# Eleven weight tiles of layer 1 split beside layer 0's output product and kept in DRAM, and norms without GpSimd

## The chip, the cores and the metric

The kernel runs on one core of a Trainium2 chip. The metric is the device time of one execution in microseconds. Before the change its median is 986.33 us over three runs (985.83 to 986.64). One further execution was profiled; all readings of the profile are from that one.

The core's engines are named as in the profile: PE is TensorE (PEld its weight loads), DVE is VectorE, ACT is ScalarE, POOL is GpSimd, SP is SyncE, which here only issues transfers. L12 is line 12 of the kernel before. Each engine runs its own instructions in order; an instruction that waits holds up what stands behind it on its engine.

## The reference

A decoder trunk of two layers on x of 1024 positions by 1024 channels, batch 1. Every layer is RMSNorm, a shift and scale computed from the conditioning vector c (adaLN), a mixer, a gate from c, and a residual add.

```python
# layer 0: gated multi-scale causal pooling, width 2048
u, z = split(h @ w_in, 2)
p = causal_multiscale_pool(u)                     # trailing means over 2, 4, 8, 16 minus u
y = einsum('bsgc,gcd->bsgd', p, w_group) * scale
x = x + gate * ((y * silu(z)) @ w_out)
# one K/V from the stream after layer 0, with a norm and shift/scale of its own
k, v = split(modulate(rmsnorm(x)) @ w_kv)
# layer 1: sliding-window attention (window 128), 16 heads on 2 K/V heads, sinks, T5 bias
q, z = split(h @ b_w_in, 2)
o = softmax_with_sink(q @ k.T / 8 + bias, masked) @ v
x = x + gate * ((o * silu(z)) @ b_w_out)
return rmsnorm(x, final_g)
```

The products have to be accurate to about float32. So the kernel splits every operand into a high part (rounded to the format fp32r that TensorE takes) and a low part, the remainder in the same format, and makes three matmuls for one: high by high, high by low, low by high.

## The kernel before

**Layout.** Channels lie on the 128 partitions and positions along the free axis, so x is eight tiles `xk[k]` of 128 by 1024. Positions are worked on in two halves q of 512. A weight tile is 128 by 1024 float32, 512 KB in DRAM: eight blocks of 128 by 128.

**Splitting a weight tile** is `load_w` (L133): `fetch` (L126) asks SP's queue for the tile into a `raw` buffer (two of them), `split_w` (L119) makes `wh`, the rounded copy, on ACT (L121) and `wl`, the remainder, on DVE (L123). `wh` and `wl` have two buffers each. A tile that is used for both halves of the positions in layer 1 is fetched and split twice.

**Layer 0's output product** (the loop over `order`, from L835) goes over 16 pairs (n, hf): eight output tiles n, each of two contraction halves hf. One step is 48 matmuls (8 blocks, 3 passes, both q) for n below `LATE` = 5, and 24 (q = 0 alone) for the rest; the q = 1 part of tiles 5 to 7 is done afterwards by `last_chunk`, in a plan by times. Beside the product lie the last adaLN dots, `ada_step` (L249): each of the 48 has one 512 KB load into a `tmp` buffer (three of them) on SP's queue and one DVE product with a sum (`ada_dot`, L238; the profile has two records for it, at L239). `ADA` says how many are written behind each step. Also beside it: parts of the gated activations come back from DRAM (`gather`), x is read again (`again_x`), and after the second half of each n `residual` (L684) and `square_add` (L197) run. For this loop the order is written for PE alone; on the other engines the framework's scheduler orders the work.

**Norms.** For a product's input x is multiplied by the reciprocal root `rb`, scaled and shifted and split. The class `Modulated` has two ways. `fold_h`/`fold_l` do it with two DVE instructions (L892, L898) and one ACT pass (L894); the first half of the positions uses it. The second half uses `step`: a DVE product (L177), an ACT pass for the high part (L159), an ACT pass in place (L163) and a POOL subtraction (L167). `prepare` (L1303) hands these steps out over time with gaps from `PREP`.

**Layer 1** is a list `specs` of products over one weight tile each: for either half q and each of four head groups r, two of queries and two of gates, then the output parts. Between them stands the attention of 32 blocks (`attend`, L1086): scores on PE, mask and maximum on DVE (L1107, L1111), exponentials on ACT (L1115), the division on DVE (L1119), transposes on PE (L1125), a cast on ACT and a remainder on DVE (L1128, L1129), two affine selects on POOL that cut the band (L1134, L1137, in 28 blocks), the product with V on PE (L1148, L1149), and the gating. `attend` is a generator, resumed by a modelled PE clock; between scores and transposes, and between transposes and the product with V, a lag of 6.0 us is written (`LAGS`). While one product runs, the next one's tile is loaded and split by `load_w`. PE's order is written; the others are scheduled by the framework. The last part of the output weights, `wbo[1]`, is used for q = 0 by `project_out(0, 1)` and once more by `out_quarter`, for which `load_last` (L1218) makes a second, lasting copy with its remainder on POOL. `stats` and `finish` make the last norm and write out.

Of the kernel before, what the change touches and what calls it, by code (L numbers as in the profile page):

```python
# [18 lines left out]
P = 128  # L19
D = 1024  # L20
T = 1024
H = 512
# [23 lines left out]
ADA = (0, 0, 0, 2, 4, 4, 4, 4, 4, 4, 1, 1, 1, 1, 0, 0)  # L46
# [9 lines left out]
def trunk(ctx, tc, xT, c, pack, ada_first, ada_rest, wu0_in, wg0_in, wa, wg, wao, wkv,  # L56
# [9 lines left out]
    pp = ctx.enter_context(tc.tile_pool(name="psum", bufs=1, space=PSUM))  # L66

# [67 lines left out]

    def rstd_stats(sq, n, more=None):
# [20 lines left out]

    def mod_h(xn, a, b, h):
        nc.scalar.activation(h, xn, AF.Identity, bias=b, scale=a)  # L159

    def mod_l(xn, a, b, h, l, f_eng=None, l_eng=None):
        if f_eng is nc.scalar:
            nc.scalar.activation(xn, xn, AF.Identity, bias=b, scale=a)  # L163
        else:
            nc.vector.tensor_scalar(out=xn, in0=xn, scalar1=a, scalar2=b,
                                    op0=ALU.mult, op1=ALU.add)
        (l_eng or nc.gpsimd).tensor_sub(out=l, in0=xn, in1=h.bitcast(F32))  # L167

    def split_mod(xn, a, b, h, l, f_eng=None):

        mod_h(xn, a, b, h)
        mod_l(xn, a, b, h, l, f_eng)

    def xn_tile(k, q, rb, xn=None):
        if xn is None:
            xn = sp.tile([P, H], F32, tag="xn", name="xn", bufs=5)
        nc.vector.tensor_mul(out=xn, in0=xk[k][:, half(q)], in1=rb)  # L177
        return xn
# [39 lines left out]
    with ExitStack() as sa:  # L218
# [580 lines left out]
        with tc.manual_schedule(engines={ET.PE}):  # L799
# [37 lines left out]
            ws, outs = {}, {}  # L837
            ws[0, 0] = half_w(0, 0)
            gather(4, 5, 6, 7)
            for i, (n, hf) in enumerate(order):  # L840
                if i + 1 < len(order):
                    ws[order[i + 1]] = half_w(*order[i + 1])
                if i == 0:
                    gather(8, 9)
                    new_x()
                    again_x(0)
                    gather(10, 11, 12, 13)
                elif i < 8:
                    again_x(i)
                qs = (0, 1) if n < LATE else (0,)  # L850
                if hf == 0:
                    outs[n] = [next_bank() for _ in qs]
                passes([(q, outs[n][q]) for q in qs], ws[n, hf], 0, g_acts(hf), KT,
                       hf == 0, hf == 1)
                for _ in range(ADA[i]):
                    ada_step()
                if hf == 1:
                    for q in qs:
                        residual(n, q, outs[n][q], 16)
# [572 lines left out]
```

## Time and profile before

| | |
|---|---|
| median of 3 runs | 986.33 us |
| the profiled execution's own time | 984.87 us |
| its span, first to last instruction | 982.6 us |
| granted TensorE clock | 0.996 |
| busy: PE, DVE, ACT, POOL | 961.9, 775.7, 458.1, 145.0 us |
| read from and written to HBM | 111.22 and 13.63 MB |
| output product of layer 0, as far as the loop goes | 423.69 to 565.13 us |
| attention layer | from about 600 us to the end |

The span is shorter than the execution's time by what lies before the first and after the last instruction. A matmul's end is modelled, so PE's busy time says where it stood still, but not how far it is from its peak. A wait is put down to the event that ended it.

### The profile page before, as it was taken

What the parts mean: (1) busy time and instruction counts of PE and PEld (TensorE: products, weight loads), DVE (VectorE), ACT (ScalarE), POOL (GpSimd) and SP (SyncE); (2) the same over time, 40 slices, a digit from 0 to 9 for tenths busy, and PEclk for the clock granted to TensorE, in tenths of its full rate; (3) what the DMA queues carried; (4) which work ended last, traced back from release to release, by engine and by line L of the source; (5) the groups of instructions that cost most, each with busy time, mean ns of one, the idle gap of its engine ahead of it and who ended that gap; (6) DMA issues with size and microseconds to landing.
All of it is one profiled execution on the core that took longest, in us unless ns stands there. A gap on an engine that the chain in (4) does not pass through costs nothing.

```text
span 982.6 us, 12696 instructions
## 1 busy us (share of the span) xinstructions
PE 961.9 (98%) x4538; PEld 801.2 (82%) x4538; DVE 775.7 (79%) x1411; ACT 458.1 (47%) x902; POOL 145.0 (15%) x173
## 2 busy tenths in 40 slices
PE   8999999999999999999999999999999999999996
PEld 6788888888888887888888888877888888887786
DVE  5897978677978699676782278599899878889985
ACT  6534434333433244551111145486677546566544
POOL 2100000000000000000000000052324313335723
PEclk9999999999999999999999999999999999999998
DMA  9453622264225411779861223222211221223222
GB/s 331 183 174 114 192 103 65 78 201 150 65 85 194 150 64 57 262 267 327 305 216 65 86 64 130 86 65 69 82 66 64 87 86 65 64 88 106 86 87 86
DMA packets 40625, 125.67 MB, mean 128 GB/s; under 512 B 4465, under 2 KB 6641, under 8 KB 40434
## 3 DMA queue, kind: packets, MB, share of 16 engines
q1 hardware_dynamic: 40416, 123.82, 37.6%
q10 hardware_dynamic: 146, 1.05, 0.3%
q8 instruction: 35, 0.57, 0.2%
q14 instruction: 28, 0.23, 0.1%
HBM read 111.22 MB, written 13.63 MB: 127 GB/s over the span
## 4 chain that ended last, share of the span: by engine, by line
PE 78%; DVE 16%; issue 2%; ACT 2%; POOL 1%; DMA 0%; POOLq 0%; DVEq 0%; SPq 0%; ACTq 0%
PE ps_d L214 14%; PE ps_S L214 9%; PE ps_d L636 9%; PE ps_d L203 6%; PE ps_d L204 6%; PE ps_d L205 6%; PE ps_S L636 4%; PE ps_o L214 4%; PE ps_tp L214 3%; DVE wl L123 2%; PE ps_d L374 2%; PE ps_o L636 2%; PE ps_tp L636 2%; DVE tmp L542 2%; PE ps_tp L1125 1%
## 5 line engine op out<-in xcount | busy, mean ns | idle before, releaser
L121 ACT CAST wh<-raw 128x1024 fp32r<-128x1024 f32 x73 | 76.5, 1048 | 101.4 <-PE ps_d L214 78.5
L123 DVE TENSOR_TENSOR wl<-raw,wh 128x1024 fp32r<-128x1024 f32 x73 | 94.2, 1290 | 26.7 <-ACT wh L121 22.8
L203 PE MATMUL ps_d<-hm,wh 128*128 128x512 f32 x288 | 113.8, 395 | 0.0
L205 PE MATMUL ps_d<-hm,wl 128*128 128x512 f32 x288 | 112.4, 390 | 0.3 <-DVE wl L123 0.3
L204 PE MATMUL ps_d<-hm,wh 128*128 128x512 f32 x288 | 112.4, 390 | 0.0
L239 DVE CUSTOM_DVE_ANT_0 tmp<-tmp,cact,pk 128x1024 f32<-128x1024 f32 x48 | 60.7, 1282 | 33.2 <-DMA tmp<-ada_rest 32.9
L214 PE MATMUL ps_d<-gh,wh 128*128 128x512 f32 x224 | 82.0, 389 | 0.0
L214 PE MATMUL ps_S<-gh,wh 128*128 128x512 f32 x192 | 64.5, 390 | 0.0
L205 PEld LDWEIGHTS ps_d<-hm,wl 128*128 128x128 f32 x288 | 54.1, 188 | 12.6 <-DVE wl L123 1.1
L636 PE MATMUL ps_d<-hs,ws 128*128 128x512 f32 x264 | 63.4, 389 | 0.0
L1115 ACT ACTIVATE pt<-pt,nm 128x129 f32<-128x129 f32 x128 | 50.2, 394 | 26.8 <-DVE nm L1111 24.6
L203 PEld LDWEIGHTS ps_d<-hm,wh 128*128 128x128 f32 x288 | 54.1, 188 | 10.2
L204 PEld LDWEIGHTS ps_d<-hm,wh 128*128 128x128 f32 x288 | 54.2, 188 | 10.0
L636 PEld LDWEIGHTS ps_d<-hs,ws 128*128 128x128 f32 x264 | 49.5, 188 | 10.3
L542 DVE TENSOR_TENSOR tmp<-tmp 128x1039 f32<-128x1039 f32 (+3 forms) x40 | 49.4, 1235 | 6.8 <-ACT tmp L672 5.7
L612 ACT CAST ws<-tw 128x512 fp32r<-128x512 f32 x44 | 26.8, 621 | 53.9 <-PE ps_tp L214 15.1
L636 PE MATMUL ps_d<-ha,ws 128*128 128x512 f32 x216 | 51.9, 389 | 0.0
L534 POOL MEMSET tmp<- 128x16 f32 x16 | 1.7, 111 | 331.4 <-DVE tmp L542 115.9
L214 PEld LDWEIGHTS ps_d<-gh,wh 128*128 128x128 f32 x224 | 42.1, 188 | 8.7
L636 PEld LDWEIGHTS ps_d<-ha,ws 128*128 128x128 f32 x216 | 40.5, 188 | 8.4
L147 POOL TENSOR_TENSOR rs<-v,mhalf 128x4 f32<-128x4 f32 (+1 forms) x7 | 8.2, 1164 | 241.6 <-DVE v L145 241.6
L214 PE MATMUL ps_d<-gh,wl 128*128 128x512 f32 x112 | 43.6, 389 | 0.0
(294 smaller groups left out, 2492.0 us busy)
## 6 DMA issues: line engine op xcount, KB each, us to landing
tmp<-ada_rest SPq DMA_DIRECT2D x48, 512.0 KB, 4.7
raw<-wb SPq DMA_DIRECT2D x32, 512.0 KB, 3.3
raw<-wa SPq DMA_DIRECT2D x28, 512.0 KB, 3.7
raw<-wao SPq DMA_DIRECT2D x20, 512.0 KB, 4.1
ad<-ada_first SPq DMA_DIRECT2D x16, 512.0 KB, 5.0
x<-xT SPq DMA_DIRECT2D x32, 256.0 KB, 5.9
raw<-wbo SPq DMA_DIRECT2D x16, 512.0 KB, 3.3
kept_g<-tmp SPq DMA_DIRECT2D x14, 512.0 KB, 2.9
```

What stands on the lines that cost most here:

```text
L121: nc.scalar.copy(out=wh, in_=raw)
L123: nc.vector.tensor_sub(out=wl, in0=raw, in1=wh.bitcast(F32))
L203: mm(ps, lh, acts(k, 0), start=k == 0, stop=False)
L204: mm(ps, lh, acts(k, 1), start=False, stop=False)
L205: mm(ps, ll, acts(k, 0), start=False, stop=k == n - 1)
L214: mm(p, lhs, acts(k, hl, q), start=start and k == 0 and s == 0, stop=stop and k == n - 1 and s == 2)
L239: nc.vector.tensor_tensor_reduce(out=raw, in0=raw, in1=ca, scale=0.5, scalar=pk[:, bcol:bcol + 1], op0=ALU.mult, op1=ALU.add, accum_out=ad ...
L374: mm(psu[i, q], w0[k // 2][:, k % 2, w, i * P:(i + 1) * P], block(k, q)[hl], start=k == 0 and s == 0, stop=k == KT - 1 and s == 2)
L542: nc.vector.tensor_add(out=nx[:, 2 * s - 1:], in0=cur[:, 2 * s - 1:], in1=cur[:, s - 1:PAD + T - s])
L612: nc.scalar.copy(out=ws[i][:, 0, :], in_=src)
L636: mm(ps, lhs, acts(k, hl), start=start and k == 0 and s == 0, stop=k == 3 and s == 2, skip_group_check=True)
L1115: nc.scalar.activation(pt[:, i, :P + 1], pt[:, i, :P + 1], AF.Exp, bias=nm[:, i:i + 1], scale=-1.0, accum_out=den[:, i:i + 1])
```

## The change

The diff has four parts.

- **The output product is cut in two.** The first six steps (`BESIDE`) stay as they were, with 24 adaLN dots written behind them instead of 10. For the last ten steps the order is now written for all five engines. In each, the next tile is split, the tile after it asked for, and then a few jobs follow from `JOBS`: an A is an adaLN dot, an S splits one of eleven tiles of `wb`. Both load into a `tmp` buffer on POOL's queue; three are asked for before the first is used, and each job that is done asks for one more. An S makes its high part in one of two `stage` buffers, its low part in place, and writes both to DRAM through POOL's queue (`keep`).
- **Layer 1 takes its tiles ready where they are kept.** `load_any` replaces `load_w`: a kept tile comes back as two transfers on POOL's queue, two products ahead instead of one, into pairs of buffers taken in turn from `raw`, `wh` and `wl`. A tile that is not kept is loaded by SP and split as before, and then kept through SP's queue, so that the second half of the positions finds it. `wbo[1]` is split once, into the lasting copy.
- **The norms of the second half** use `fold_h`/`fold_l`.
- **The output parts** come in another order: `project_out(1, 0)[:2]` before `project_out(0, 1)`, and `stats(0)` and `finish(0, 4)` one product later.

```diff
-ADA = (0, 0, 0, 2, 4, 4, 4, 4, 4, 4, 1, 1, 1, 1, 0, 0)
+ADA = (0, 0, 2, 6, 8, 8)
+BESIDE = 6
+JOBS = ("AAS", "AAS", "SSA", "SSA", "S", "S", "S", "S", "S", "")
...
+    def keep(key, hi, lo, queue=nc.sync):
+        kept_w[key] = [kp.tile([P, 1024], F32, name="kw") for _ in range(2)]
+        for dst, src in zip(kept_w[key], (hi, lo)):
+            queue.dma_start(dst, src.bitcast(F32))
+    def pair_tiles():
+        tags = (("raw", "raw"), ("wh", "wl"), ("wh", "wl"))[turns[0] % 3]
+        turns[0] += 1
+        return [wp.tile([P, 1024], F32R, tag=t, name="w2") for t in tags]
...
+            staged = [1, 8, 9, 2, 3, 10, 11, 4, 5, 12, 13]
+            def ask():
+                if not jobs:
+                    return
+                raw = tmp()[:, :1024]
+                kind = jobs.pop(0)
+                if kind == "A":
+                    i = rest_at[0]
+                    nc.gpsimd.dma_start(raw, ada_rest[i])
+                    rest_at[0] += 1
+                    asked.append(lambda: ada_dot(raw, cact, *rest_cols[i]))
+                else:
+                    i = staged.pop(0)
+                    nc.gpsimd.dma_start(raw, wb[i])
+                    asked.append(lambda: stage_split(i, raw))
+            def stage_split(i, raw):
+                hi = stage_hi[i % 2].rearrange("p a c -> p (a c)")
+                nc.scalar.copy(out=hi, in_=raw)
+                lo = raw.bitcast(F32R)
+                nc.vector.tensor_sub(out=lo, in0=raw, in1=hi.bitcast(F32))
+                keep(("b", i), hi, lo, nc.gpsimd)
...
+        with tc.manual_schedule(engines={ET.PE, ET.Activation, ET.DVE, ET.Pool, ET.SP}):
+            stage_hi = [slot("stage") for _ in range(2)]
+            raw = fetch(wao[order[BESIDE + 1]])
+            jobs, asked = list("".join(JOBS)), []
+            for _ in range(3):
+                ask()
+            for i in range(BESIDE, len(order)):
+                if i + 1 < len(order):
+                    ws[order[i + 1]] = split_w(*raw)
+                if i + 2 < len(order):
+                    raw = fetch(wao[order[i + 2]])
+                if i < KT:
+                    again_x(i)
+                for _ in JOBS[i - BESIDE]:
+                    asked.pop(0)()
+                    ask()
+                out_half(i)
...
+            if key in again:
+                keep(again[key], *w)
+        again = {"wk": ("kv", 0), "wv": ("kv", 1), "wq": ("b", 0)}
...
-    def load_last():
...
+    def load_any(key):
+        stays = key[0] == "o" and key[1] == 1
+        if stays:
+            t = hp.tile([P, 2, T], F32R, tag="h", name="wo")
+            w = t[:, 0, :], t[:, 1, :]
+            last_w.append(w)
+        else:
+            w = pair_tiles()
+        if key in kept_w:
+            for dst, src in zip(w, kept_w[key]):
+                nc.gpsimd.dma_start(dst, src)
+        else:
+            raw = bp.tile([P, 1024], F32, tag="raw1", name="raw1", bufs=2)
+            nc.sync.dma_start(raw, (wb if key[0] == "b" else wbo)[key[1:]])
+            nc.scalar.copy(out=w[0], in_=raw)
+            nc.vector.tensor_sub(out=w[1], in0=raw, in1=w[0].bitcast(F32))
+            if not stays:
+                keep(key, *w)
+        return w
...
             for k in ks:
-                m.step(k)
+                m.fold_h(k, sp.tile([P, H], F32, tag="xn", name="xn", bufs=5))
+                m.fold_l(k)
                 yield gap
...
-        *woven(project_out(0, 1) + project_out(1, 0)[:2], (0, 2, 4, 6)),
-        stats(0), project_out(1, 0)[2], finish(0, 4, FINISH[0]),
-        *project_out(1, 0)[3:],
+        *project_out(1, 0)[:2],
+        *project_out(0, 1),
+        project_out(1, 0)[2], stats(0), project_out(1, 0)[3], finish(0, 4, FINISH[0]),
+        project_out(1, 0)[4],
...
-        loaded = {srcs[0]: got["wq"]}
+        loaded = {srcs[0]: got["wq"], srcs[1]: load_any(specs[srcs[1]][0])}
...
-                nxt = srcs.index(i) + 1
+                nxt = srcs.index(i) + 2
                 if nxt < len(srcs):
-                    loaded[srcs[nxt]] = load_w(specs[srcs[nxt]][0])
+                    loaded[srcs[nxt]] = load_any(specs[srcs[nxt]][0])
```

More of the change, by code (lines that the diff above doesn't have):

```diff
@@ L156, in rstd_spread @@
         return bc
[L158 to L178, printed above, removed]
     sqh = [None, None]
@@ L1177, in run @@
                 yield from gemm_steps(w, i * 512, acts, 4, done)
-        return wbo[part, n2], run
+        return ("o", part, n2), run
     def bare(f):
```

70 lines of the change are left out of this document (24 added, 46 removed).

## The prediction

> **What bounds the kernel now.** I read the page first (sections 1 and 4), then the stages one by one, then the waits of TensorE, then the chain of waits inside the stages that lose time.
>
> ```profile
> span 982.6 us, 12696 instructions
> ...
> PE 961.9 (98%) x4538; PEld 801.2 (82%) x4538; DVE 775.7 (79%) x1411; ACT 458.1 (47%) x902; POOL 145.0 (15%) x173
> ...
> PE 78%; DVE 16%; issue 2%; ACT 2%; POOL 1%; DMA 0%; POOLq 0%; DVEq 0%; SPq 0%; ACTq 0%
> ```
>
> TensorE bounds the kernel, and its number of matmuls does not change. So the change can win only where TensorE waits, and it loses wherever it makes a new wait. The stages it touches are the output product of layer 0 (423.69 to 565.13) and layer 1 (from about 600):
>
> ```profile
> 423.69:488.97 65.28, 65.28 (x289) 54.05 (x288) 45.93 (x69) 16.44 (x25) 0.00 (x0) 1.00 0.90 313
> 488.97:532.49 43.52, 43.52 (x193) 36.04 (x192) 22.78 (x36) 6.75 (x9) 0.00 (x0) 1.00 0.50 165
> 532.49:565.13 32.64, 32.64 (x145) 27.03 (x144) 11.32 (x13) 7.43 (x9) 0.00 (x0) 1.00 0.25 81
> ...
> 600.00:640.00 40.00, 39.73 (x196) 33.35 (x195) 27.44 (x55) 20.88 (x41) 3.73 (x5) 1.00 0.36 118
> 640.00:690.00 50.00, 46.21 (x231) 38.09 (x230) 47.33 (x103) 36.91 (x78) 22.22 (x20) 1.00 0.23 74
> 690.00:740.00 50.00, 49.59 (x249) 41.28 (x248) 46.26 (x120) 37.95 (x89) 18.30 (x19) 1.00 0.23 74
> 740.00:880.00 140.00, 140.00 (x700) 118.14 (x699) 117.68 (x296) 83.99 (x211) 39.94 (x46) 1.00 0.22 72
> 880.00:935.00 55.00, 52.19 (x269) 43.28 (x268) 51.16 (x113) 31.95 (x77) 37.20 (x28) 1.00 0.31 96
> ```
>
> The columns are the stretch, its length, then busy time of PE, PEld, DVE, ACT and POOL, the granted clock, the DMA share and GB/s. The output product loses nothing: ten halves, of which the four from 488.97 take 10.88 us each (43.52 / 4) and the last six 5.44 (32.64 / 6), with DVE, ACT and the DMA engines half idle in them. Layer 1 loses 0.27 + 3.79 + 0.41 + 2.81 = 7.28 us of TensorE, and DVE is busy 95% and 93% just there. What TensorE waits for:
>
> ```profile
> PE ps_tp L1125 <- DVE pt L1119: 6.1, 5, 1.6
> PE ps_tp L154 <- DVE cur L1129: 0.4, 1, 0.4
> PE ps_d L205 <- DVE wl L123: 0.3, 1, 0.3
> PE ps_S L1105 <- DVE qt L1063: 0.3, 1, 0.3
> ```
>
> Eight waits, all for DVE, six of the seven us for the softmax division. The chain of waits from 640 to 690 and from 880 to 935 says what DVE did instead:
>
> ```profile
> by line: DVE wl L123 16.5%; DVE xn L177 12.4%; DVE pt L1111 8.8%; DVE ps_S L1107 7.0%; DVE cur L1129 6.9%; DVE pt L1119 6.7%; DVE of L1155 6.5%; issue 5.0%; POOL hm L167 4.8%; DVE qt L1063 4.1%; DVE qt L1161 3.2%; DVE of L1159 2.9%; DVE KL
> ...
> by line: DVE wl L123 14.7%; DVE of L1159 9.7%; DVE of L1155 8.6%; ACT pt L1115 8.3%; DVE cur L1129 7.4%; DVE x L686 7.4%; issue 6.1%; DVE pt L1111 5.6%; DVE ps_S L1107 5.5%; ACT wh L121 5.2%; DVE pt L1119 4.3%; DVE qt L1161 3.7%; DVE szb L1
> ```
>
> In both, the low half of a weight split (L123) is the largest item, 8.2 and 8.1 us, and the matmuls hardly appear: there the chain runs along DVE.
>
> **The change part by part.** *Splits leave layer 1.* Today layer 1 splits 45 tiles on DVE and four of wbo once more on POOL; afterwards 12 are split there (four of wb, the eight of wbo), and 33 come ready from DRAM as two transfers.
>
> ```profile
> L123 DVE TENSOR_TENSOR wl<-raw,wh 128x1024 fp32r<-128x1024 f32 x45 | 60.0, 1334 | 12.2 <-ACT wh L121 9.9 <-PE ps_o L1149 1.7
> L177 DVE TENSOR_TENSOR xn<-x,rb 128x512 f32<-128x512 f32 x16 | 12.5, 809 | 0.4 <-POOL hm L167 0.3
> L898 DVE SCALAR_TENSOR_TENSOR hm<-tmp,adac,hm 128x512 fp32r<-128x512 f32 x4 | 2.9, 744 | 0.0
> L1129 DVE TENSOR_TENSOR cur<-ps_tp,cur 128x512 fp32r<-128x512 f32 x32 | 22.1, 690 | 7.1 <-ACT cur L1128 6.3
> ...
> L121 ACT CAST wh<-raw 128x1024 fp32r<-128x1024 f32 x45 | 47.0, 1045 | 15.2 <-issue 7.6 <-PE ps_d L204 6.4 <-ACT qt L1062 0.9
> L1128 ACT CAST cur<-ps_tp 128x512 fp32r<-128x512 f32 x32 | 18.8, 587 | 11.0 <-PE ps_tp L1125 10.4
> ...
> L1134 POOL TENSOR_SCALAR_AFFINE_SELECT prev<-cur 128x1024 fp32r<-128x1024 f32 x28 | 33.3, 1189 | 46.8 <-DVE cur L1129 46.8
> L1137 POOL TENSOR_SCALAR_AFFINE_SELECT cur<-cur 128x1024 fp32r<-128x1024 f32 x28 | 32.5, 1160 | 1.8
> L167 POOL TENSOR_TENSOR hm<-xn,hm 128x512 fp32r<-128x512 f32 x16 | 22.4, 1403 | 24.9 <-ACT xn L163 22.6 <-DVE wl L123 2.3
> ```
>
> 33 x 1.334 = 44.0 us leave DVE, 33 x 1.045 = 34.5 us leave ACT. *The norms.* Each of the 16 tiles of normalized input had one DVE product (0.81), two ACT passes and one subtraction on POOL (1.40). It gets two DVE instructions of the kind of L898 (0.744 each, 1.49) and one ACT pass: DVE +0.68, POOL -1.40. Layer 1 as a whole loses 44.0 - 10.9 = 33 us of DVE work, but the two edits do not meet in the same place:
>
> ```profile
> 640.00:690.00 50.00, 8.62 (x6) 1.00 0.23 74
> 880.00:935.00 55.00, 9.79 (x7) 1.00 0.31 96
> ...
> 640.00:690.00 50.00, 10.40 (x13) 1.00 0.23 74
> ```
>
> (Busy time of L123 in the two stretches, then of L177 in the first.) From 640 to 690 six splits leave, 8.62 us, but 13 of the 16 norms lie there: 10.40 us become 13 x 1.49 = 19.4, so DVE gains 0.35 us of work, not relief. What does leave is POOL's subtraction, which stretches DVE's product:
>
> ```profile
> 644.76 1.77 DVE L177 TENSOR_TENSOR xn<-x,rb 128x512 f32<-128x512 f32 x1 [0.34 <-POOL hm L167]
> ...
> 642.35 3.64 POOL L167 TENSOR_TENSOR hm<-xn,hm 128x512 fp32r<-128x512 f32 x2 [7.06 <-ACT xn L163]
> ```
>
> Beside a POOL subtraction the DVE product took 1.77 us instead of its mean 0.81. The gain in this stretch lies between 0 (DVE as full as before) and 3.79; the chain gives up its 2.4 us of POOL (4.8%) and keeps the 0.35, so I take 1.5, nearer to zero because those 2.4 us overlap the stretched DVE instruction. From 880 to 935 three of seven splits leave (four tiles of wbo are still split there), 4.2 us, and POOL's four subtractions of those tiles move to ACT and DVE's ordinary split; a norm does not stand there. Of 2.81 I take 2.1 (bounds 0 and 2.81). The two neighbours: 0.5 of 0.68. Each wait also hides about 0.16 us under the modelled end of a matmul (0.39 shown, one issued every 10.88 / 48 = 0.227): 8 x 0.16, of which 0.4. Sum of the gain: **4.5 us** (0 to 7.3 + 1.3).
>
> *Reloads* cost layer 1 nothing if they are in time: a tile is asked for two products ahead (2 x 24 x 0.227 = 10.9 us at least), one transfer takes 3.3 us (row below), and 33 x 1.05 + 11 x 1.05 MB instead of 33 x 0.52 adds 29 MB to 380 us, 76 GB/s on top of 72 to 118. What they cost when POOL is late is the second rival.
>
> *The eleven tiles beside the output product.* Some prices, and how many dots DVE had done by 489 and in the 25 us after (a dot leaves two records):
>
> ```profile
> 423.69:489.00 65.31, 24.91 (x39) 1.00 0.90 313
> 489.00:514.00 25.00, 13.13 (x22) 1.00 0.74 244
> ...
> 495.27 1.21 DVE L123 TENSOR_TENSOR wl<-raw,wh 128x1024 fp32r<-128x1024 f32 x1
> ```
>
> From 488.97 on, every engine follows the written order: 17 jobs, 0 to 16, in the order A A S, A A S, S S A, S S A, S, S, S, S, S over nine halves. A is an adaLN dot (one load, one DVE dot), S a tile (one load, ACT copy 1.05, DVE subtraction 1.21 undisturbed, two writes). DVE has room: 11 x 1.21 = 13.3 us in 76. The DMA engines have little, and the POOL queue less. Bytes: 17 loads, 22 writes, 8 tiles of wao and 1 MB of x, 49 x 0.524 = 25.7 MB in 76.2 us, 337 GB/s. The most that the engines moved in any half of the product:
>
> ```profile
> 456.33:467.21 10.88, 10.88 (x49) 9.01 (x48) 7.83 (x13) 2.28 (x4) 0.00 (x0) 1.00 0.98 345
> ...
> raw<-wb SPq DMA_DIRECT2D x32, 512.0 KB, 3.3
> kept_g<-tmp SPq DMA_DIRECT2D x14, 512.0 KB, 2.9
> ```
>
> So one transfer occupies 0.524 / 345 = 1.52 us, and a write lands 2.9 - 1.52 = 1.38 after its bytes. Now the queue: loads and writes of the jobs all go through POOL, in order. There are three `tmp` buffers, all asked for ahead; the load asked after job j takes j's own buffer, so POOL stands until j's low half has landed, and the next tile's two writes stand behind it. One tile therefore costs a full cycle: load + two writes + landing, 3 x 1.52 + 1.38 = 5.9 us, and 7.5 when SP's tile of wao shares the engines (+1.52). That is over the 5.44 us of a late half, and S S A needs 13.4 to 16.4 against 10.88. Only the start made earlier can pay. Job 15 must be done before the last half's tile is split, and its load waits for the write of job 12: five cycles after the write of job 5 (jobs 6, 7, 9, 10, 12) plus the loads of 11 and 14 (3.0). Job 5's write lands at 509 at best: 499.85, when half 6 ends and frees a buffer, + split 2.26 + two dots of 1.28 + subtraction 1.21 + write 2.9. At worst DVE enters late: 24 dots stand ahead of the stage now, 20 were done by 489, and four more at the old pace (25 / 11 = 2.27) end at 498; split, two dots and job 2 with both its writes (1.2 + 2.6 + 2.3 + 4.4) give 508.5, job 5's load, split and writes (3.3 + 2.3 + 4.4) 518. Then load 3.3, copy 1.05, two subtractions 2.42. Best: 509 + 29.7 + 3.0 + 6.8 = 548.5, 11 us early, no stall. Worst by these rows: 518 + 37.3 + 3.0 + 6.8 = 565.1 against 560.1 (last half at 559.7, its low weights 0.4 later): 5.0 us of stall. I take **2.5**, the middle: the DMA share of the six halves before, 0.90, speaks for the long cycle, the loads made ahead for the short one.
>
> [...] No row of before has a transfer issued by POOL.
>
> What one POOL issue costs is bounded by POOL's rows: 0 and L167's 1.40 us. Inside a cycle the issues overlap the bytes, so the sum takes 0 and the third rival 1.40.
>
> **Sum.** 984.87 is the profiled execution's own time (982.6 + 2.27 around the span), 1.46 under the median 986.33. -4.5 + 2.5 = -2.0: 982.9 profiled, **984.3** by the median. That is the size of what this kernel's measurement tells from nothing (0.2%, 2 us).
>
> **The rivals.** *One, the stage hides it all:* the first writes land near 509 and the output product stalls nowhere. For it: 76 us in which DVE is 45% and ACT 19% busy. Against: 337 of 345 GB/s. 986.3 - 4.5 = 981.8. *Two, POOL in layer 1:* the 66 reloads stand in POOL's queue with the affine selects of the 28 masked blocks. A reload waits for the product before to free its buffers, and behind it stand L1134 and L1137, for whose 2.35 us the weighted values on TensorE wait; the slack is the written lag of 6.0 us less cast, subtraction and selects (0.59 + 0.69 + 2.35), 2.4. Two issues at 1.40 exceed it by 0.4: 5.6 us if half the blocks are hit, 984.3 + 5.6 = 989.9. For: POOL is busy 37 of 55 us from 880. Against: it loses L167's 22.4 us. *Three, slower, one mechanism:* each cycle of the stage carries one unhidden POOL issue. At 7.46 + 1.40 = 8.9 us the last tile is ready at 518 + 44.3 + 9.8 = 572.1, 12 us late; -4.5 + 12 = +7.5, **993.8**. It decides from a cycle of about 7.8, where the stall passes 6.5 and the sum passes +2.
>
> **How the numbers follow.** Forecast 0.35 (own range 981 to 987: 0.18 past 2 us faster, 0.16 within, 0.01 slower), rival one 0.22, two 0.15 (0.05 of it within, if few blocks are hit), three 0.23, something else 0.05 (0.02, 0.01, 0.02). Faster: 0.18 + 0.22 + 0.02 = 0.42. Same: 0.16 + 0.05 + 0.01 = 0.22. Slower: 0.01 + 0.10 + 0.23 + 0.02 = 0.36. The range takes in one with the upper bound of the gain and three: 977 to 995.
>
> **What would show it.** The windows of the last ten halves: PE busy below its length, first from the fifth half on, with waits for L123's or the stage's subtraction; POOL's waits there are for landings of the kept tiles, 6 to 7.5 us apart. In 640 to 690 DVE still over 90% and the wait for L1119 smaller by a third only; in 880 to 935 PE idle under 1 us. No L167, no L177. I am wrong if TensorE loses nothing before 600 (cycle shorter than 5.9), if 640 to 690 loses nothing (the port, not the work, was the limit), or if TensorE waits for a reload.

## The result, and the profile after

The changed kernel takes 1000.42 us (median of 5, 998.02 to 1002.21) against 986.64 for the kernel before (median of 5): a ratio of 1.0139, 95% interval 1.0123 to 1.0155. It is 1.4% slower where 0.2% faster was forecast, and outside the range. The profiled execution is the fastest of the five, 998.02. Medians and ratios below leave out one execution of the run with the norms alone, which took 3451.69 us at a granted clock of 1.00.

The page of the changed kernel, its span, busy time and chain by engine:

```profile
span 996.3 us, 12788 instructions
...
PE 965.5 (97%) x4538; PEld 803.8 (81%) x4538; DVE 748.5 (75%) x1405; ACT 422.2 (42%) x860; POOL 163.9 (16%) x258
...
PE 67%; DVE 14%; DMA 7%; issue 7%; ACT 2%; POOL 2%; POOLq 0%; SPq 0%; DVEq 0%; ACTq 0%
```

DVE lost 27 us of work, ACT 36, and the span grew by 13.7 us all the same. PE is busy 3.6 us longer with the same 4538 matmuls, so some of them ran slower. DMA, 0% of the chain before, is 7% of it now. By stretch (PE, PEld, DVE, ACT, POOL, then granted clock, DMA share, GB/s):

```profile
489.15:532.67 43.52, 43.52 (x193) 35.96 (x192) 24.72 (x32) 10.18 (x12) 10.49 (x19) 1.00 0.80 277
532.67:584.30 51.63, 38.21 (x145) 29.72 (x144) 21.21 (x22) 14.56 (x16) 10.77 (x20) 0.83 0.79 281
619.00:659.00 40.00, 40.00 (x197) 33.64 (x197) 22.56 (x51) 16.02 (x36) 9.35 (x17) 1.00 0.82 288
659.00:708.00 49.00, 48.00 (x242) 39.97 (x241) 43.98 (x112) 27.12 (x72) 17.28 (x27) 1.00 0.39 130
708.00:757.00 49.00, 49.00 (x246) 41.16 (x245) 46.76 (x116) 33.19 (x80) 10.93 (x14) 1.00 0.59 215
757.00:896.00 139.00, 138.53 (x693) 116.75 (x692) 98.86 (x282) 63.81 (x187) 53.45 (x76) 1.00 0.47 154
896.00:949.00 53.00, 51.02 (x262) 43.10 (x261) 39.94 (x111) 25.49 (x70) 26.50 (x28) 1.00 0.23 74
```

The four long halves of the output product still take 43.52 us. The six short ones take 51.63 instead of 32.64: **19.0 us lost**, 13.4 of them idle (51.63 - 38.21) and 5.6 in which PE is busy longer (38.21 - 32.64). Most of the 5.6 is matmuls that ran slower: the granted clock is 0.50 while PE works from 548.39 to 554.59 and from 578.48 to 581.90, and half of these 9.6 us is 4.8. The rest is not accounted for; modelled ends can hide some of it. Layer 1 from 619 on has 0 + 1.00 + 0 + 0.47 + 1.98 = 3.45 us of idle PE where the same stretches had 7.28. By the span it gives back 19.0 + 0.2 (the later start of the first of these halves) - 13.7 = 5.5 us, the rest of it under modelled ends and in the last norm.

What PE waits for, first from 489 to 585 and then from 600 to 960:

```profile
PE ps_S L211 <- ACT wh L126: 12.9, 2, 10.1
PE ps_S L211 <- DVE wl L128: 0.5, 1, 0.5
...
PE ps_tp L1158 <- DVE pt L1152: 2.7, 3, 2.0
PE ps_d L201 <- DVE hm L943: 0.8, 1, 0.8
```

In the stage it is two waits for the high half of an output weight (L126 is the split's cast, L121 before): 10.1 us before half 11, the second of the short ones, and 2.8 before half 15, the last. In layer 1 the softmax division, 6.1 us before, is down to 2.7. PE nowhere waits for a reload.

Why was that cast late? It stands in ACT's and DVE's written order behind the jobs of step 9 and the residual of half 9. DVE in time, around the 10 us wait (start, duration, instruction, idle before it):

```profile
541.69 1.23 DVE L858 TENSOR_TENSOR tmp<-tmp,stage 128x1024 fp32r<-128x1024 f32 x1 [5.08 <-ACT stage L856]
544.13 1.28 DVE L236 CUSTOM_DVE_ANT_0 tmp<-tmp,cact,pk 128x1024 f32<-128x1024 f32 x1 [1.22 <-DMA tmp<-ada_rest]
...
545.34 0.75 DVE L683 SCALAR_TENSOR_TENSOR x<-ps_o,adac,x 128x512 f32<-128x512 f32 x1
546.00 0.74 DVE L683 SCALAR_TENSOR_TENSOR x<-ps_d,adac,x 128x512 f32<-128x512 f32 x1
546.78 1.35 DVE L192 TENSOR_TENSOR sqh<-sqh,sq 128x512 f32<-128x512 f32 x2
548.38 1.23 DVE L128 TENSOR_TENSOR wl<-raw,wh 128x1024 fp32r<-128x1024 f32 x1 [0.24 <-ACT wh L126]
```

DVE has time, it idles 5.08 and 1.22 us. It waits for a staged tile (L858) and then for a dot's load; only after them come the residual, its squares (ACT's, ahead of L126) and the split. Both loads were late on POOL: the tile's, issued at 531.87 behind two writes, was there for its cast at 540.61, and the dot's was issued at 539.72, after POOL had stood still for 7.31 us. Some of POOL's transfers in time, POOL's waits for landings from 489 to 585, and the median time from issue to landing:

```profile
512.28 1.79 POOL L850 DMA_DIRECT2D tmp<-wb  x3 [8.13 <-DMA kw<-tmp]
...
539.72 0.55 POOL L845 DMA_DIRECT2D tmp<-ada_rest  x1 [7.31 <-DMA kw<-tmp]
...
564.58 0.55 POOL L850 DMA_DIRECT2D tmp<-wb  x1 [7.05 <-DMA kw<-tmp]
565.18 0.53 POOL L147 DMA_DIRECT2D kw<-stage  x1
565.78 0.53 POOL L147 DMA_DIRECT2D kw<-tmp  x1
574.13 0.55 POOL L850 DMA_DIRECT2D tmp<-wb  x1 [7.82 <-DMA kw<-tmp]
```

```profile
POOL tmp L850 <- DMA kw<-tmp: 30.7, 4, 8.1
POOL tmp L845 <- DMA kw<-tmp: 11.0, 2, 7.3
```

```profile
w<-kw POOLq DMA_DIRECT2D x66, 512.0 KB, 4.2
...
tmp<-wb POOLq DMA_DIRECT2D x11, 512.0 KB, 4.6
kw<-stage POOLq DMA_DIRECT2D x11, 512.0 KB, 6.0
kw<-tmp POOLq DMA_DIRECT2D x11, 512.0 KB, 7.2
```

Here is the predicted cycle: a load is issued when the low half of an earlier tile has landed, the next tile's two writes follow it at once, and POOL stands still again, for 7 to 8 us in five of the eight cases and for 3.7 to 5.5 in the others. From the load after the first write (512.28) to the load after the eighth (574.13) are seven cycles, **8.8 us each**. An issue takes 0.54 us, but the low half lands 7.2 us after its own, where 2.9 was put in.

### The profile page after: what moved, and what is told of

Same layout as the page of the kernel before. It is cut to its first block, busy times and chain, and to the rows that moved or that the text cites. A ratio compares the mean times of both kernels' runs of the same rounds, so it can differ in the third digit from the quotient of the medians.

```text
span 996.3 us, 12788 instructions
## 1 busy us (share of the span) xinstructions
PE 965.5 (97%) x4538; PEld 803.8 (81%) x4538; DVE 748.5 (75%) x1405; ACT 422.2 (42%) x860; POOL 163.9 (16%) x258
## 3 DMA queue, kind: packets, MB, share of 16 engines
q0 software_dynamic: 15120, 55.06, 16.4%
## 4 chain that ended last, share of the span: by engine, by line
PE 67%; DVE 14%; DMA 7%; issue 7%; ACT 2%; POOL 2%; POOLq 0%; SPq 0%; DVEq 0%; ACTq 0%
PE ps_d L633 9%; PE ps_d L200 8%; PE ps_d L201 8%; PE ps_d L202 8%; PE ps_d L211 7%; PE ps_S L211 5%; PE ps_S L633 4%; DMA tmp<-ada_rest 3%; PE ps_d L371 2%; PE ps_o L633 2%; PE ps_tp L211 2%; PE ps_tp L633 2%; DVE tmp L539 2%; PE ps_o L211 2%; DVE tmp L236 1%
## 5 line engine op out<-in xcount | busy, mean ns | idle before, releaser
L200 PE MATMUL ps_d<-hm,w 128*128 128x512 f32 x264 | 104.5, 396 | 0.0
L201 PE MATMUL ps_d<-hm,w 128*128 128x512 f32 x264 | 103.1, 391 | 0.8 <-DVE hm L943 0.8
L202 PE MATMUL ps_d<-hm,w 128*128 128x512 f32 x264 | 102.9, 390 | 0.0
L211 PE MATMUL ps_S<-gh,wh 128*128 128x512 f32 x192 | 68.0, 410 | 12.9 <-ACT wh L126 12.9
L202 PEld LDWEIGHTS ps_d<-hm,w 128*128 128x128 f32 x264 | 49.6, 188 | 10.6
L201 PEld LDWEIGHTS ps_d<-hm,w 128*128 128x128 f32 x264 | 49.7, 188 | 10.2 <-DVE hm L943 1.2
L200 PEld LDWEIGHTS ps_d<-hm,w 128*128 128x128 f32 x264 | 49.6, 188 | 9.2
L211 PEld LDWEIGHTS ps_S<-gh,wh 128*128 128x128 f32 x192 | 37.8, 199 | 21.6 <-ACT wh L126 13.7
L1262 POOL DMA_DIRECT2D w<-kw x66 | 35.8, 543 | 92.0 <-PE ps_d L202 56.0
L126 ACT CAST wh<-raw 128x1024 fp32r<-128x1024 f32 x28 | 29.4, 1050 | 38.7 <-PE ps_d L211 31.3
```

The lines of the kernel that those rows point to most:

```text
L126: nc.scalar.copy(out=wh, in_=raw)
L200: mm(ps, lh, acts(k, 0), start=k == 0, stop=False)
L201: mm(ps, lh, acts(k, 1), start=False, stop=False)
L202: mm(ps, ll, acts(k, 0), start=False, stop=k == n - 1)
L211: mm(p, lhs, acts(k, hl, q), start=start and k == 0 and s == 0, stop=stop and k == n - 1 and s == 2)
L1262: nc.gpsimd.dma_start(dst, src)
```

## The experiments

Every profiled stage length below runs from the start of half 6 to the end of half 15; it is 76.16 us in the kernel before.

**The writes on SP.**

```
-                keep(("b", i), hi, lo, nc.gpsimd)
+                keep(("b", i), hi, lo)
```

> The changed kernel with one word changed: the two writes of each staged tile go out on SP's queue, the loads stay on POOL's. Bytes, jobs and buffers are the same. Theory 1 (POOL's order): POOL stands for the landing of a tile's low half with the next tile's writes behind it, 8.1 + 3.7 + 7.3 + 7.7 + 7.1 + 7.8 us in the changed kernel. With the writes elsewhere a buffer's own round (load 4.2, copy 1.05, subtraction 1.22, writes about 5) is all that is left, some 12 us over three buffers, 4 us a tile, under the 5.44 of a late half: the 19.0 us that the ten halves lost fall to 0 to 4, and the time to 981 to 986. Theory 2 (bytes): 25.7 MB in 76 us is what the DMA engines carry at most, and who asks does not matter: at least 14 of the 19 us stay, 995 or more. Theory 3 (the place of the jobs in ACT's and DVE's order): the next half's split stands behind jobs whose loads are late for either reason; it goes with theory 1 or 2 and isn't told apart here.

989.45 (median of 5), 1.0048 (1.0031 to 1.0065) of before. Profiled at 984.15, the fastest of its runs; the stage, the waits of PE in it, and the landings:

```profile
488.67:569.90 81.23, 78.42 (x338) 63.87 (x336) 44.91 (x54) 24.89 (x28) 9.41 (x17) 0.98 0.90 332
```

```profile
PE ps_S L211 <- ACT wh L126: 1.9, 1, 1.9
```

```profile
kw<-stage SPq DMA_DIRECT2D x11, 512.0 KB, 4.2
kw<-tmp SPq DMA_DIRECT2D x11, 512.0 KB, 5.2
```

One argument of a call takes the loss in the stage from 19.0 to 5.1 us in the profiled executions (two waits of 0.9 us together for a low half are the rest of PE's idle time there), and 11.0 us off the median. The same bytes now move at 332 GB/s instead of some 280, so the bytes were not the limit: the rival falls for most of the loss. The median is 3.5 us above what theory 1 allowed. The other four runs, all near 990, show a granted clock of 0.989 to 0.994 against 0.996, which points to more waiting than in the profiled one; where, no profile of them shows.

**Two loads ahead instead of three.**

```
-            for _ in range(3):
+            for _ in range(2):
                 ask()
```

> The changed kernel with two loads asked ahead of the jobs instead of three, all on POOL's queue as before. Then the load asked after job j takes the buffer of job j-1, whose writes were issued one job earlier, and the writes of job j stand ahead of it and not behind. Theory 1 (POOL stands for a landing that it has only just asked for): the waits for landings shrink from about 7 us to 0 to 3 each although fewer loads are ahead; a tile's cycle falls from 8.6 us to 5 to 6.5, the loss of the ten halves from 19 us to 2 to 8, the time to 984 to 991. Theory 2 (bytes): no change, 998 to 1002. A rival of both: the loads ahead were what hid the load's 4 us, and one fewer makes it slower still, over 1002.

991.95 (median of 4), 1.0076 (1.0048 to 1.0104), just past the upper end of theory 1:

```profile
488.11:577.32 89.21, 79.15 (x338) 64.52 (x336) 46.18 (x54) 24.86 (x28) 21.27 (x39) 0.94 0.87 308
```

```profile
PE ps_S L211 <- ACT wh L126: 10.0, 1, 10.0
```

The order in POOL's queue counts: with one load fewer ahead, POOL waits 12.6 us for landings instead of 41.7, and 13.0 us are lost instead of 19.0. But the wait before half 11 is the same 10 us. Reordering one queue moves the loss about; it does not remove it.

**Nothing staged.** The eleven tiles are split in layer 1, at their first use.

```
-JOBS = ("AAS", "AAS", "SSA", "SSA", "S", "S", "S", "S", "S", "")
+JOBS = ("AA", "AA", "A", "A", "", "", "", "", "", "")
-            staged = [1, 8, 9, 2, 3, 10, 11, 4, 5, 12, 13]
+            staged = []
```

> The changed kernel without the eleven staged tiles: the ten halves have their six dots and nothing else, and layer 1 splits those eleven tiles at their first use, keeps them, and takes them ready for the second half. Norms, order of the parts and reloads as changed. The stage should lose nothing (0 to 1 us, no drop of the granted clock), so the time tells what the rest of the change is worth without the relief of 600 to 690: I expect 640 to 690 to lose more than before, since six splits of 1.3 to 1.4 us come back onto DVE next to 13 norms of 1.49 us (4 to 9 us lost instead of 3.8), and 880 to 935 to lose 1 to 2 instead of 2.8: 985 to 991. The rival, that POOL's subtractions and not DVE's load made the waits there: 980 to 984.

988.22 (median of 10), 1.0033 (1.0019 to 1.0047). The stage takes 76.15 us: all 19 us belong to the eleven tiles. What is left of the change, reloads and norms without the staging, costs some 3 us, and layer 1 from 655 to 700 shows why:

```profile
655.00:700.00 45.00, 41.10 (x189) 33.88 (x190) 40.32 (x99) 25.89 (x65) 8.71 (x12) 0.92 0.41 144
```

3.9 us of PE idle and a granted clock below 1: the new norms and the splits stand in the same place. That is the first theory; the rival (980 to 984) falls.

**The norms alone**, put into the kernel before.

```
-                m.rb, m.act = state["rb"], True
+                m.rb = state["rb"]
             for k in ks:
-                m.step(k)
+                m.fold_h(k, sp.tile([P, H], F32, tag="xn", name="xn", bufs=5))
+                m.fold_l(k)
```

> The kernel before with the norms of the second half made by two DVE instructions and one ACT pass, nothing else. Load theory (what DVE has to do sets 640 to 690): 13 norms add 13 x 0.65 = 8.4 us to a stretch in which DVE is busy 47.3 of 50 us, so TensorE loses 4 to 8 us more there: 989 to 994. Port theory (POOL's subtractions stretch DVE's instructions, 1.77 for 0.81): those go, DVE's stretched time falls by 3 to 5 us and TensorE loses 0 to 3 us less: 983 to 987.

990.70 (median of 3), 1.0055 (1.0038 to 1.0071), as the load theory has it and not the port theory ("port", here and in the prediction, is a name for the stretch that is measured below; that a port makes it, no run shows). From 640 to 690 (prediction: PE 46.21, DVE 47.33):

```profile
640.00:690.00 50.00, 43.86 (x203) 36.10 (x202) 47.60 (x104) 28.11 (x61) 8.38 (x10) 0.93 0.20 64
```

```profile
PE ps_S L1105 <- DVE ps_S L1101: 4.9, 1, 4.9
```

DVE is as full as before, with more to do, and PE waits 4.9 us at once. POOL's subtractions did stretch DVE's products (in the kernel before 1.77 us beside one, at 644.76, where the mean was 0.81), but 0.7 us more per tile on DVE is dearer than that.

**Seven tiles, writes on SP.** The other four tiles are split in layer 1.

```
-JOBS = ("AAS", "AAS", "SSA", "SSA", "S", "S", "S", "S", "S", "")
+JOBS = ("AAS", "AAS", "SA", "SA", "S", "S", "S", "", "", "")
-            staged = [1, 8, 9, 2, 3, 10, 11, 4, 5, 12, 13]
+            staged = [1, 8, 9, 2, 3, 10, 11]
-                keep(("b", i), hi, lo, nc.gpsimd)
+                keep(("b", i), hi, lo)
```

> Seven tiles staged instead of eleven (one beside each of seven halves, none in the last three), their writes on SP's queue; the other four are split at their first use in layer 1, between about 700 and 800 us, where TensorE waited for nothing. Theory 1 (the stage lost its 19 us to the chain of 8.6 us per tile on POOL's queue, and the tiles that are ready help layer 1): halves 6 to 15 within 1.5 us of 76.2, no granted clock under 1 there, layer 1 keeps some 4 of its 5.3 us: 980 to 984. Rival (what is left in the run with all eleven writes on SP, 5 us in the stage, comes from bytes or from SP's own queue, not from the number of tiles): 3 us or more lost in the stage, 985 to 990.

984.59 (median of 11), 0.9990 (0.9981 to 1.0000): not to be told from no change, and 0.6 us above theory 1. The stage is as forecast (76.17 us, clock 1.00 throughout). Layer 1 is what falls short. From 660 to 680, and DVE in time there:

```profile
660.00:680.00 20.00, 17.85 (x83) 14.31 (x82) 18.58 (x43) 10.77 (x27) 3.62 (x6) 0.91 0.59 203
```

```profile
670.72 1.22 DVE L1267 TENSOR_TENSOR w<-raw,w 128x1024 fp32r<-128x1024 f32 x1
...
671.94 0.72 DVE L943 SCALAR_TENSOR_TENSOR hm<-xn,adac,hm 128x512 fp32r<-128x512 f32 x1
```

One tile that is no longer staged is split in the midst of the norms (L1267 ahead of L943): PE waits 1.9 us for L943, and the clock is at half for 3.4 us after.

**Seven tiles, writes on POOL.** As above, with `keep(("b", i), hi, lo, nc.gpsimd)`.

> The same seven tiles with the writes left on POOL's queue. Theory 1, a rate: seven cycles of 8.6 us are 60 us, under the 76 us of the ten halves, and step 9 has one tile and one dot instead of two tiles and one dot in front of half 11's split, so at most 2 us are lost there: 980 to 985. Rival, a place: whatever the count, a job that waits for a landing on POOL's queue holds up the next half's split, so the late halves of 5.44 us lose 3.2 us each where a tile of 8.6 us stands in front: three late halves with a tile, some 9 us, 989 to 993.

985.14 (median of 11), 0.9991 (0.9981 to 1.0000), 0.1 us past the upper end of theory 1; the stage takes 76.39 us, 0.2 lost. The low half lands hardly sooner than with eleven (6.9 us in the median against 7.2), but seven cycles of the changed kernel's 8.8 us are 62 us and fit. The rate theory holds: it is the number of cycles, not the waiting as such; three of the short halves have a tile in front here, and 0.2 us is all that is lost.

**Seven tiles and the old norms.** As the run with seven on SP, with `prepare` making the norms as before the change (product on DVE, two passes on ACT, POOL's subtraction).

> As the run with seven tiles and writes on SP, with the norms of layer 1's second half made as before: one product on DVE, two passes on ACT, the subtraction on POOL. [...]

984.57 (median of 11; 980.26 to 986.50), 0.9983 (0.9970 to 0.9997): the median of the new norms. Neither kind is dearer here: in its profile PE idles 2.69 us from 645 to 665 at a mean clock of 0.91, where with the new norms it idles 2.15 from 660 to 680, also at 0.91. In these two profiles the one cost replaces the other.

**Waits made on purpose.** On the kernel with nothing staged, idle subtractions go ahead of the splits for halves 11, 13 and 15.

```
+SLOW = {10: 4, 12: 6, 14: 9}
+                if i in SLOW:
+                    z = tmp()[:, :1024]
+                    nc.vector.memset(z, 0.0)
+                    for _ in range(SLOW[i]):
+                        nc.vector.tensor_sub(out=z, in0=z, in1=z)
```

> Nothing staged, and 4, 6 and 9 idle subtractions of 1.2 us put on DVE ahead of the splits for halves 11, 13 and 15: extra work that computes nothing used, to make TensorE wait there. A split has about 3 us to spare (5.44 less 2.3), so waits of about 2, 4 and 8 us. What it tells apart: that the granted clock of 0.5 answers to a wait and to its length (0.5 from some 2.5 us into each wait that is that long, for as long again or longer, and a half then takes up to 3 us more), or that it came from the stage's traffic (no clock below 1 here at all).

1017.38 in one run. The waits were 4.1, 6.1 and 7.2 us, the first two longer and the last shorter than meant. The stretches are cut where the recorded clock changes:

```profile
540.80:546.50 5.70, 1.61 (x7) 1.05 (x6) 5.48 (x5) 0.84 (x1) 0.00 (x0) 1.00 0.06 11
546.50:549.90 3.40, 3.40 (x9) 2.67 (x8) 0.00 (x0) 0.00 (x0) 0.00 (x0) 0.50 0.81 281
...
560.10:570.30 10.20, 6.12 (x14) 4.79 (x15) 5.09 (x5) 0.00 (x0) 0.00 (x0) 0.50 0.32 103
...
584.00:594.20 10.20, 6.08 (x14) 4.78 (x15) 4.00 (x4) 0.00 (x0) 0.00 (x0) 0.50 0.15 51
```

No tile is staged, in the two long half-clock stretches only 103 and 51 GB/s move, and the clock halves after each wait: for 3.4 us after the one of 4.1, for 10.2 us around the one of 6.1 (and 10.2 again around 7.2). So the halving answers to the waiting. That it begins 2.5 us into a wait does not hold: after the first wait PE had resumed at 545.27, and the clock halved at 546.50, 1.2 us later. Two later waits of this run, 2.2 us at 596 and 2.7 at 924, left the clock at 1.00; the last section takes them up.

**Nine tiles, writes on SP.** As the run with seven, with `"S"` in two more steps.

```
-JOBS = ("AAS", "AAS", "SA", "SA", "S", "S", "S", "", "", "")
+JOBS = ("AAS", "AAS", "SA", "SA", "S", "S", "S", "S", "S", "")
-            staged = [1, 8, 9, 2, 3, 10, 11]
+            staged = [1, 8, 9, 2, 3, 10, 11, 4, 5]
```

> Nine tiles staged, one beside each of nine halves, writes on SP's queue; six tiles of wb are split in layer 1. With seven tiles a split stood on DVE at 670.7 among the norms, and TensorE waited 2.1 us there and ran 3.4 us at half clock: 4.4 us in all. Theory 1 (that split is what is left over in that place): with nine it is gone, 660 to 700 loses under 2.5 us and the stage under 1.5, so 981 to 984. Rival (the eleven-tile run on SP lost 5 us in the stage for its bytes, and nine are nearer to eleven than to seven): the stage loses 3 us or more, 985 to 988.

**982.17** (median of 6, 981.77 to 983.62) against 985.76: 0.9969 (0.9958 to 0.9981). It beats both kernels. The stage, then the two stretches of layer 1:

```profile
489.33:565.50 76.17, 76.17 (x338) 63.07 (x337) 43.41 (x52) 22.69 (x26) 8.31 (x15) 1.00 0.89 320
660.00:680.00 20.00, 19.03 (x95) 15.44 (x94) 19.53 (x47) 9.87 (x28) 6.37 (x10) 1.00 0.50 159
880.00:900.00 20.00, 17.64 (x78) 14.68 (x77) 14.54 (x41) 8.33 (x24) 6.86 (x9) 0.91 0.49 154
```

The product loses nothing at 320 GB/s, and from 660 to 680 PE idles 1.0 us instead of 2.15, at full clock: theory 1 holds. What is left is near 889: a split of the last output weights on DVE (L1267, 1.20 us) ahead of the division, 2.4 us of wait and a stretch at half clock.

**That last split on POOL.** As with nine tiles, and:

```
-            nc.vector.tensor_sub(out=w[1], in0=raw, in1=w[0].bitcast(F32))
+            (nc.gpsimd if stays else nc.vector).tensor_sub(out=w[1], in0=raw,
+                                                           in1=w[0].bitcast(F32))
```

> As the run with nine tiles, with the low halves of the last four tiles of the output weights subtracted on POOL, as before the change. Theory 1 (the wait near 889, 2 to 2.7 us in every kernel of the changed kind, is DVE's subtraction of such a tile that stands in front of the softmax division): it falls to about the 1.7 us of before and without a half-clock stretch; 880 to 900 loses 1 to 2 us instead of 2.2 to 4.2: 1 to 2 us faster than the run with nine tiles. [...]

```profile
880.00:900.00 20.00, 19.22 (x97) 15.97 (x96) 15.94 (x39) 10.66 (x28) 16.16 (x14) 1.00 0.63 198
```

In the profiled run (981.04) the wait near 889 is 0.8 us, no longer for the division, and the clock stays at 1.00, so the place was named rightly. But the median is 983.77, with runs from 979.04 to 986.19 (0.9968, 0.9952 to 0.9984): no gain over nine tiles that these runs can tell, and a wider spread whose cause they do not show.

**Nine tiles and the old norms.**

> As the run with nine tiles, with the norms of layer 1's second half made as before (DVE product, two ACT passes, POOL subtraction). With seven tiles the two kinds of norms gave the same time, 984.6. Theory 1 (with the splits staged the kind of norm does not matter): within 1 us of the run with nine tiles. Rival (POOL's subtraction is the cost that remains, 2.85 us of wait at 654 with DVE's product at 1.76 us, or DVE's added load is): 2 us or more apart.

983.43 (median of 11, 980.84 to 986.95), 0.9985 (0.9971 to 0.9999); 1.3 us above nine tiles with the new norms, between the two theories' bounds. Its profiled run (986.65, near the top of its runs) waits 2.7 us for a division near 655 and 3.4 near 890. With the splits out of the way the new norms are not worse and perhaps a little better.

**Nine tiles, writes on POOL.** As with nine tiles, with `keep(("b", i), hi, lo, nc.gpsimd)`.

> As the run with nine tiles, with the writes left on POOL's queue as the change has them: what of the 15 us between that run and the changed kernel is the number of tiles, what the queue. Theory 1, a rate of 8.6 us per tile on POOL's queue: the first write lands near 512, the sixth near 555, the load asked for behind it (the ninth tile's) lands near 560 and is split near 562, some 3 us after the last half wanted the split behind it; steps 8 and 9 have one tile each, so half 11 waits under 1 us: 2 to 5 us lost in the stage, all in the last two or three halves, and 984 to 988. Rival (only the two steps with two tiles each made the stall, whatever the queue): nothing lost in the stage, 981 to 983.5.

987.62 (median of 11, 982.15 to 991.82), 1.0012 (0.9992 to 1.0032). The stage up to 554, and from there its last two halves:

```profile
489.00:554.00 65.00, 64.59 (x284) 52.87 (x284) 38.54 (x47) 18.91 (x22) 14.28 (x26) 1.00 0.81 281
554.00:571.00 17.00, 14.15 (x55) 10.90 (x54) 5.08 (x6) 3.66 (x4) 3.75 (x7) 0.90 0.77 289
```

The stage takes 82.16 us (488.59 to 570.75), a loss of 6.0 (theory 1 allowed 5), most of it at the end and with a stretch at half clock, as a chain that is late by a little would make it. The rival falls: no step has two tiles here, and the stage loses all the same. Between this kernel and the one with nine tiles on SP, one argument, lie 5.5 us of median (the kernel before differs by 0.4 between the two sets of runs).

Put side by side, the profiled stage loses 0.2, 6.0 and 19.0 us with seven, nine and eleven tiles when the writes go through POOL's queue, and 0, 0 and 5.1 us when they go through SP's. Count and queue both matter.

## Why the prediction was wrong

*The gain in layer 1 was right as a sum.* 4.5 us were put down, 5.5 came. By place it was less good: 640 to 690 gave 2.8 of its 3.79 (I took 1.5), 880 to 935 only 0.8 of 2.81 (I took 2.1). That two errors of opposite sign met is luck. The reason for the second is the wait that the nine-tile runs show: a split of the last weights, which stays on DVE, ahead of the division. The changed kernel has it too (L1267 from 905.60 to 906.79, ahead of the division that ends PE's wait of 2.0 us). The gain from 640 to 690 comes from the staging and not from the norms: without staged tiles that place loses more than before, and the norms alone cost 5 us. Costing the norms there at "0.35 us of work" was right only beside six splits that leave.

*The stall in the output product is the step that failed:* 2.5 us, with bounds from 0 to 5.0; it measured 19.0. The mechanism was the one described, POOL held at a landing with the next tile's writes behind it. Three things in its sum were wrong.

- *The cycle.* "One tile therefore costs a full cycle: load + two writes + landing, 3 x 1.52 + 1.38 = 5.9 us, and 7.5" is 8.8. The 1.52 is 0.524 MB at the highest rate of any half of the product and the 1.38 an estimate, what is left of the 2.9 us in which the writes of before landed. Three transfers issued 0.6 us apart beside SP's load landed after 4.6, 6.0 and 7.2 us in the median. A worst case built from the best rate and a median landing is no worst case. Job 2's low half landed at 511.9, not by 508.5, and job 5's at 522.5, not by 518 at the latest.
- *The place.* I checked only whether the last half's split was in time. The first to be late was half 11: steps 8 and 9 have two tiles each, and the text had said that such a step needs 13.4 to 16.4 us against 10.88. What it did not follow up is what stands behind those jobs in DVE's and ACT's written order: half 9's residual, its squares, and the split that PE needs.
- *The clock.* No term was there for matmuls that run slower after a wait. It is 4.8 of the 19.0 us, by the half-clock stretches above.

*The rivals.* The third (a longer cycle on POOL's queue, 8.9 us, 993.8) was nearest: its cycle is right within 0.1 us. Its cause is not; it had 1.40 us per POOL issue, and an issue takes 0.54. The extra time is in the landings. The second (reloads in POOL's queue delaying the selects) didn't come: PE has no wait for a reload or, in the changed kernel, for a select. The first (the stage hides it all, 981.8) is near what nine tiles on SP do, at 982.17; for eleven on POOL's queue it is refuted.

*What stays open in part:* why a write from POOL's queue took 6.0 to 7.3 us in the median in this stage (5.4 and 5.8 with two loads ahead) and the same write from SP's 4.2 to 5.4. By the mean of the stage the DMA share was 0.80 with the one and 0.90 with the other, but the mean hides bursts. Around the landing of job 7's low half (issued at 531.24, landed at 539.3), and in a pause some us later:

```profile
536.00:539.00 3.00, 2.29 (x11) 1.56 (x9) 0.61 (x1) 0.00 (x0) 0.00 (x0) 1.00 1.03 421
546.00:547.00 1.00, 0.00 (x0) 0.00 (x0) 0.96 (x3) 0.85 (x2) 0.95 (x3) 0.50 0.00 0
```

While that write was under way the DMA engines were full for 3 us, with four POOL transfers, issued from 530.11 to 531.87, and SP's tile of wao (530.87) on the way; at 546 they stood empty. So a part of the late landing is the burst's own bytes (an estimate: five transfers, 2.6 MB, take 6.2 us at 421 GB/s). How much is left for the queue itself these runs do not separate. The reloads of layer 1, as large and on the same queue, landed after 4.2 us in the median and 3.3 at least in the changed kernel, so the low halves' 7.2 does not come with the queue alone.

## What to carry to other kernels

When work is moved to a queue that waits for its own landings, cost the cycle from landings under the load that the change itself makes, compare cycles times tiles with the stretch that covers them, and check every consumer behind the jobs in each engine's written order, not the last one alone. Nine tiles instead of eleven, with their writes on another queue, made the difference here between 0.3% faster and 1.4% slower. And price a new wait of TensorE of about 2 us or more at more than its length: of the 17 waits of 1.9 to 2.8 us in the table below, 12 went with 3.4 us at half clock.

## What the runs showed of the hardware

TensorE's granted clock fell to 0.50 during or just after waits of 1.4 to 10.1 us, and stayed there for 3.4, 6.8, 10.2 or 13.7 us, whole multiples of 3.4. Waits and the half-clock stretches that went with them (the first 45 us and the last norm, where the end of the execution cuts the stretch off, are left out, and so are waits under 1.5 us that left the clock alone, but for the longest of a kernel):

| kernel | wait of TensorE, us | at half clock, us |
|---|---|---|
| before | 1.6 (longest, near 655 and 666) | none |
| changed | 10.1; 2.8; 2.0 | 13.7; 3.4; none |
| writes on SP | 1.9; 2.4 | 3.4; none |
| two ahead | 10.0; 2.2 | 10.2; 3.4 |
| norms alone | 4.9; 1.5 | 6.8; none |
| seven tiles, SP | 1.9; 2.6 | 3.4; 3.4 |
| seven tiles, POOL | 1.9; 1.9 | 3.4; none |
| seven tiles, old norms | 2.7; 2.3 | 3.4; 3.4 |
| nothing staged | 1.4; 1.1 and 1.4 close together | 3.4; 3.4 |
| waits on purpose | 4.1; 6.1; 7.2; 2.2; 2.7 | 3.4; 10.2; 10.2; none; none |
| nine tiles, SP | 2.4 | 3.4 |
| the same, last split on POOL | 0.8 (longest) | none |
| nine tiles, old norms | 2.7; 3.4 | 3.4; 3.4 |
| nine tiles, POOL | 2.3; 2.7 | 3.4; 3.4 |

Between 1.4 and 2.7 us the same length did it once and not another time, even within one run (seven tiles on POOL). In the traces it goes with where the wait lies. Within each of the 14 profiles all recorded changes of the clock (64 in all) lie whole multiples of 3.413 us apart, to 0.003 us (before: 8.473 and 974.445, 283 of them apart; changed: 8.457, 540.936, 554.590, 578.483, 581.896 and 991.496, that is 156, 4, 7, 1 and 120). In each profile they stand on one grid with cells of 3.413 us, whose place against the start of the kernel differs from profile to profile: its first edge is at 1.65 us before, 1.63 in the changed kernel, 1.43 with seven tiles on POOL. Here are the two waits of 1.9 us with seven tiles on POOL, cut on that grid:

```profile
670.44:673.85 3.41, 1.50 (x7) 0.94 (x6) 3.41 (x10) 1.30 (x8) 0.22 (x1) 1.00 0.22 89
673.85:677.26 3.41, 3.41 (x9) 2.67 (x8) 3.40 (x6) 2.16 (x4) 0.00 (x0) 0.50 1.02 360
888.89:892.30 3.41, 1.70 (x8) 1.08 (x6) 3.34 (x8) 2.11 (x6) 0.00 (x0) 1.00 0.42 150
892.30:895.71 3.41, 3.23 (x20) 2.96 (x21) 3.29 (x12) 1.26 (x4) 1.41 (x2) 1.00 0.00 0
```

The first wait lies whole in one cell of the grid: PE idles 1.91 us in it (3.41 - 1.50), and the next cell runs at 0.50. The second is cut in two, 1.71 and 0.18, and the clock stays. The wait of 2.7 us among the waits on purpose was cut as well, into 1.25 and 1.46. Counted over all profiles, between 45 us and the last norm: after each of the 20 full-clock cells in which PE idled 1.9 us or more the clock was at half, after none of those in which it idled 1.72 or less, and after one of three between (1.74, 1.74 and 1.87). From half it came back after every cell in which PE idled up to 0.58 us (21 of them) and stayed after every cell with 0.61 or more (10). So the wait of 10.1 us cost four cells: it ended 0.67 us into the third, and only the fourth was idle-free. This is a count over 14 profiles of closely related kernels, with PE's modelled ends, and no more than that. It does not hold for the first 45 us, where the clock fell four times after cells with less than 0.4 us of idle time, nor for the last norm (before: the clock fell at 974.445 after a cell with 0.81 us).

At half clock a matmul was issued every 0.43 us where it was every 0.23 before (changed kernel, 550.25 to 554.09 against 536.77 to 537.91), so by an estimate a cell of 3.4 us costs up to 1.7 us more (half of it). A wait in layer 1 can thus cost more than its length. That the place of the grid adds to the spread of one kernel's runs is a guess of the author's, since each kernel has one profile: nine tiles on POOL ran from 982.15 to 991.82 us at clocks between 0.996 and 0.990, though the fastest of them was not the one with the highest clock.
